# Interleaving two tensors: from two load buffers and two output buffers to three regions woven in place

## The chip, the core and the metric

The kernel runs on one core of one Trainium2 chip. The metric is device time in microseconds (us) for one execution of the program, lower is better.

Five engines work beside each other on a core. Here VectorE (DVE in the profile) copies; SyncE (SP) and ScalarE (ACT) issue transfers, each on a queue of its own; 16 DMA engines move the data between the chip's memory (HBM) and SBUF, the on-chip memory with 128 partitions. PSUM is a second, smaller on-chip memory. The engines are held in order by semaphores: an instruction waits until a counter has reached a value, and a transfer that has landed adds 16.

## What is computed

```python
# x, y: (32, 256, 1024) float32
result = np.zeros((32, 256, 2048), dtype=np.float32)
result[..., 0::2] = x
result[..., 1::2] = y
```

Nothing is calculated. Each output row takes its even places from x and its odd places from y. Both inputs hold 33.55 MB, the output 67.11 MB, so 134.22 MB have to cross between HBM and SBUF.

## The kernel before

x, y and the output are seen as flat lists of numbers. They are cut into n = 8 tiles. A tile of x is 128 partitions by W = 8192 numbers, a row of 32 KiB in each partition (4 MiB together); a tile of y is the same, and a tile of the output is 128 by 16384 numbers. Because interleaving keeps the order of the flat lists, tile k of the output needs tile k of x and of y alone, and partition p needs nothing of other partitions.

Six buffers of 32 KiB a partition fill 192 KiB: `xt[0]` and `xt[1]` for x, `yt[0]` and `yt[1]` for y (tile k uses number k % 2), and `ot[0]` and `ot[1]` for the output. An output buffer holds half of an output tile: `ot[0]` always the first half (h = 0), `ot[1]` the second (h = 1).

Three lists of instructions run beside each other:

- **SP issues the loads** (lines 42 to 53). Tile 0 of x comes in two halves (lines 42 and 43), so that copying can begin earlier. Then, for each k, x into `xt[k % 2]` (line 50) and y into `yt[k % 2]` (line 53). From k = 2 on, each waits until VectorE has made its last copy out of that buffer for tile k - 2 (the semaphore `woven`, lines 48 and 52).
- **VectorE weaves** (lines 55 to 70). For each half of a tile there are two copies of 4096 numbers a partition: x into the even places of `ot[h]` (line 67), y into the odd places (line 70). The first copy waits for the load of x and for the store of the same half of the tile before, since that store still reads `ot[h]` (line 64); the second copy of half 0 waits for the load of y.
- **ACT issues the stores** (lines 72 to 83), one of 4 MiB for each half, with rows of 32 KiB, after the two copies of that half. The first store of all is cut into a piece of 1 MiB with rows of 8 KiB (line 77) and one of 3 MiB with rows of 24 KiB (line 81).

At the end ACT waits for the last store of half 0 and clears the semaphores with one instruction over their range (line 90), and SP waits for the last store of half 1 and takes its count back (line 91).

The wrapper `tile_interleave_kernel` moves the first two loads on SP ahead of a drain in the opening block, so that they start early. It is the same in both kernels.

Of the kernel before, what the change touches and what calls it, by code (L numbers as in the profile page):

```python
# [3 lines left out]


def _interleave(nc, x, y, out):
    P = 128
    W = 8192
    H = W // 2  # L10

    total = 1
    for s in x.shape:
        total *= s
    n = total // (P * W)
    assert n * P * W == total

    def rows(ap, names, k):
        flat = ap.rearrange("b s d -> (b s d)")
        return flat[k * names : (k + 1) * names].rearrange("(p w) -> p w", p=P)  # L20

    fp32 = mybir.dt.float32
    xt = [nc.alloc_sbuf_tensor(f"xt{b}", [P, W], fp32).ap() for b in (0, 1)]
    yt = [nc.alloc_sbuf_tensor(f"yt{b}", [P, W], fp32).ap() for b in (0, 1)]
    ot = [nc.alloc_sbuf_tensor(f"ot{b}", [P, W], fp32).ap() for b in (0, 1)]

    xsem = [nc.alloc_semaphore(f"xsem{b}") for b in (0, 1)]
    hsem = nc.alloc_semaphore("hsem")
    qsem = nc.alloc_semaphore("qsem")
    ysem = [nc.alloc_semaphore(f"ysem{b}") for b in (0, 1)]  # L30
    woven = nc.alloc_semaphore("woven")
    osem = [nc.alloc_semaphore(f"osem{b}") for b in (0, 1)]


    cuts = [0, W // 4, W]
    parts = [slice(a, b) for a, b in zip(cuts, cuts[1:])]

    xs = [rows(x, P * W, k) for k in range(n)]
    ys = [rows(y, P * W, k) for k in range(n)]
    os_ = [rows(out, 2 * P * W, k) for k in range(n)]  # L40

    nc.sync.dma_start(out=xt[0][:, :H], in_=xs[0][:, :H]).then_inc(xsem[0], 16)
    nc.sync.dma_start(out=xt[0][:, H:], in_=xs[0][:, H:]).then_inc(hsem, 16)

    for k in range(n):
        b = k % 2
        if k >= 2:
            nc.sync.wait_ge(woven, 4 * (k - 2) + 3)
        if k:
            nc.sync.dma_start(out=xt[b], in_=xs[k]).then_inc(xsem[b], 16)  # L50
        if k >= 2:
            nc.sync.wait_ge(woven, 4 * (k - 2) + 4)
        nc.sync.dma_start(out=yt[b], in_=ys[k]).then_inc(ysem[b], 16)

    for k in range(n):
        b = k % 2
        for h in (0, 1):
            c = slice(h * H, (h + 1) * H)
            if h == 0:
                nc.vector.wait_ge(xsem[b], 16 * (k // 2 + 1))  # L60
            elif k == 0:
                nc.vector.wait_ge(hsem, 16)
            if k:
                nc.vector.wait_ge(osem[h], 16 * k)
            if (k, h) == (1, 0):
                nc.vector.wait_ge(qsem, 16)
            nc.vector.tensor_copy(out=ot[h][:, 0::2], in_=xt[b][:, c]).then_inc(woven, 1)  # L67
            if h == 0:
                nc.vector.wait_ge(ysem[b], 16 * (k // 2 + 1))
            nc.vector.tensor_copy(out=ot[h][:, 1::2], in_=yt[b][:, c]).then_inc(woven, 1)  # L70

    for k in range(n):
        for h in (0, 1):
            nc.scalar.wait_ge(woven, 4 * k + 2 * h + 2)
            if (k, h) == (0, 0):
                for c in parts[:-1]:
                    nc.scalar.dma_start(
                        out=os_[k][:, c], in_=ot[h][:, c]
                    ).then_inc(qsem, 16)
                c = parts[-1]  # L80
                nc.scalar.dma_start(out=os_[k][:, c], in_=ot[h][:, c]).then_inc(osem[h], 16)
                continue
            nc.scalar.dma_start(
                out=os_[k][:, h * W : (h + 1) * W], in_=ot[h]
            ).then_inc(osem[h], 16)

    nc.scalar.wait_ge(osem[0], 16 * n)
    used = sorted(s.num for s in [*xsem, hsem, qsem, *ysem, woven, osem[0]])
    assert used == list(range(used[0], used[-1] + 1)), used
    nc.scalar.sem_clear(range(used[0], used[-1] + 1))  # L90
    nc.sync.nop(nofuse=True).wait_op(osem[1], 16 * n, "sem-ge").then_inc(
        osem[1], -16 * n
    )


def kernel(tc, x, y, out):
    nc = tc.nc
    tc.close()
    tc.compile()

    _interleave(nc, x, y, out)

    blocks = nc.main_func.blocks
    for engine in (mybir.EngineType.SP, mybir.EngineType.SP):
        opening = blocks[0].instructions
        at, moved = next(
            (b, i)
            for b in blocks[1:]
            for i in b.instructions
            if i.engine == engine and i.opcode == "DMACopy"  # L110
        )
        assert not (moved.sync_info and moved.sync_info.on_wait)
        body = at.instructions
        body.remove(moved)
        gate = next(
            n
            for n, i in enumerate(opening)
            if i.engine == engine and i.opcode == "Drain"
        )
        opening.insert(gate, moved)  # L120
        at.instructions = body
        blocks[0].instructions = opening


# [1 line left out]
_INS = ['x', 'y']  # L126
_OUTS = [((32, 256, 2048), 'float32')]


# [23 lines left out]
```

## Time and profile before

| | |
|---|---|
| time, median of 3 runs | 314.25 us (314.22 to 314.38) |
| span of the profiled execution, first to last instruction | 312.9 us |
| what the median has over this span | 1.35 us |
| VectorE busy | 72.0 us (23% of the span) in 32 copies |
| DMA | 134.22 MB, 429 GB/s over the span |
| VectorE waited for stores | 206.5 us in 14 waits |
| VectorE waited for the first loads | x 7.3 us, y 12.3 us |

The profiled execution is a separate one, taken with the hardware profiler. Its durations are set against its own span of 312.9 us; the third row says what lies around it in an unprofiled run.

How to read the profile. An engine is busy while an instruction of its own works; instructions that only wait, branch or issue a transfer don't count. The page cuts the span into 40 equal slices of 7.8 us, and a digit gives the busy share in tenths (9 is 90% or more); the DMA row is the mean over the 16 DMA engines. The chain of work that ended last is followed backwards from the last instruction: at each step to what it had waited for. A DMA in that chain stands from its issue to its landing, so it may include time in which it stood in the queue behind others. A line of the timeline reads: start, duration, engine, line of the kernel, operation, target and source, and in brackets how long the engine was idle before and what ended that. A line of the DMA issues reads: target and source, issuing queue, number of issues, KB each, and the median time from issue to landing. Beside these views the trace keeps a record of every single DMA packet, with its start, duration and bytes; a packet here is one row of one partition.

### The profile page before, as it was taken

The page shows a single profiled execution, that of the slowest core. Times are in us where ns is not written, and L with a number is a line of the kernel's source. Part 1 is how long each engine was busy: PE and PEld are TensorE (multiplying, and loading weights), DVE is VectorE, ACT ScalarE, POOL GpSimd, SP SyncE. Part 2 cuts the span into 40 slices and gives each one's busy share as a digit, 9 for nine tenths or more (in the row PEclk, how much of TensorE's full clock was granted, in tenths as well). Part 3 has the DMA queues.
Part 4 walks back from the last instruction along what each step waited for, and adds up shares of the span by engine and source line. Part 5 has one row for each costly group of instructions (what it writes and reads, how often), then busy time and mean ns, then how long its engine had stood idle before and what let it go on. Part 6 is the DMA issues. An engine that isn't in the chain of part 4 may idle for free.

```text
span 312.9 us, 114 instructions
## 1 busy us (share of the span) xinstructions
DVE 72.0 (23%) x32; POOL 0.2 (0%) x4
## 2 busy tenths in 40 slices
DVE  0216000501305023050220503205032050415410
POOL 0000000000000000000000000000000000000000
DMA  8999999999999999999999999999999999999998
GB/s 337 467 402 436 436 402 419 452 457 415 427 444 411 461 402 469 402 469 402 469 402 465 406 440 432 423 448 402 469 402 469 402 469 402 469 402 448 423 423 381
DMA packets 4896, 134.22 MB, mean 429 GB/s; under 512 B 544, under 2 KB 544, under 8 KB 544
## 3 DMA queue, kind: packets, MB, share of 16 engines
q1 hardware_dynamic: 2448, 67.11, 50.1%
q10 hardware_dynamic: 2448, 67.11, 49.7%
HBM read 67.11 MB, written 67.11 MB: 429 GB/s over the span
## 4 chain that ended last, share of the span: by engine, by line
DMA 82%; DVE 12%; issue 0%
DMA out_dram<-ot 76%; DMA yt<-in_y_dram 6%; DVE ot L70 6%; DVE ot L67 6%
## 5 line engine op out<-in xcount | busy, mean ns | idle before, releaser
L67 DVE COPY ot<-xt 128x4096 f32<-128x4096 f32 x16 | 36.7, 2295 | 213.8 <-DMA out_dram<-ot 206.5
L70 DVE COPY ot<-yt 128x4096 f32<-128x4096 f32 x16 | 36.6, 2288 | 12.3 <-DMA yt<-in_y_dram 12.3
L137 POOL MEMSET const-bfloat16-1.0<- 128x1 bf16 x1 | 0.1, 103 | 0.0
L137 POOL MEMSET const-uint8-127<- 128x1 uint8 x1 | 0.1, 102 | 0.0
L137 POOL MEMSET const-float32-0.0<- 128x1 f32 x1 | 0.1, 100 | 0.2 <-issue 0.2
L137 POOL MEMSET const-float32-1.0<- 128x1 f32 x1 | 0.1, 99 | 0.0
## 6 DMA issues: line engine op xcount, KB each, us to landing
out_dram<-ot ACTq DMA_DIRECT2D x15, 4096.0 KB, 34.1
yt<-in_y_dram SPq DMA_DIRECT2D x8, 4096.0 KB, 41.5
xt<-in_x_dram SPq DMA_DIRECT2D x7, 4096.0 KB, 24.3
xt<-in_x_dram SPq DMA_DIRECT2D x2, 2048.0 KB, 9.5
out_dram<-ot ACTq DMA_DIRECT2D x1, 3072.0 KB, 32.8
out_dram<-ot ACTq DMA_DIRECT2D x1, 1024.0 KB, 16.3
```

Source lines behind the costliest of these rows:

```text
L67: nc.vector.tensor_copy(out=ot[h][:, 0::2], in_=xt[b][:, c]).then_inc(woven, 1)
L70: nc.vector.tensor_copy(out=ot[h][:, 1::2], in_=yt[b][:, c]).then_inc(woven, 1)
L137: nc = _bacc.Bacc("TRN2", target_bir_lowering=False, num_devices=1)
```

## The change

The six buffers become three regions `R[0]` to `R[2]` of 64 KiB a partition, 192 KiB together; tile k uses region k % 3. x of a tile is loaded into the first half of its region, y into the second half, and the output tile is woven in the same 64 KiB. So that nothing is overwritten before it is read, the second half of x (4096 numbers a partition) is first parked in PSUM. The rest of the weaving is a chain of copies, each of which waits for the one before (the semaphore `step`):

1. the second half of x to PSUM (`park`);
2. the first half of x spread over the even places of the first half of the region, in pieces from the top: 2048, 1024, 512, 256, 128 and 64 numbers, and then the last 64 by way of a small buffer `last`, 8 copies;
3. the first half of y into the odd places of the first half of the region: one copy. The first half of the output tile is now done;
4. the second half of y spread over the odd places of the second half, in such pieces from the bottom, 8 copies;
5. the parked half of x from PSUM into the even places of the second half.

That is 19 copies a tile, where there were 4. Loads of a region wait until all of the stores of the tile that had it have landed. Stores have rows of 64 KiB for tiles 1 to 4 (one transfer of 8 MiB, after all 19 copies). Tiles 5, 6 and 7 are stored in two halves with rows of 32 KiB, the first one after step 3. Tile 0 is stored in three parts, with rows of 8, 24 and 32 KiB. Both halves of tile 0 of x have to be in before the first copy. The semaphores are cleared one at a time.

The core of the diff (the names of buffers and semaphores at the head are left out):

```diff
+    def copy(to, of):
+        nonlocal count
+        if count:
+            nc.vector.wait_ge(step, count)
+        nc.vector.tensor_copy(out=to, in_=of).then_inc(step, 1)
+        count += 1
+    def halvings(m):
+        while m > 64:
+            assert m % 2 == 0
+            yield m // 2, m
+            m //= 2
+        yield 0, m
...
     for k in range(n):
-        b = k % 2
-        if k >= 2:
-            nc.sync.wait_ge(woven, 4 * (k - 2) + 3)
+        b = k % REGIONS
+        X = low = R[b][:, :N]
+        Y = high = R[b][:, N:]
+        if k == 0:
+            nc.vector.wait_ge(fsem, 16)
+        nc.vector.wait_ge(xsem[b], 16 * (k // REGIONS + 1))
+        copy(park, X[:, H:])
+        for i, j in halvings(H):
+            if i:
+                copy(low[:, 2 * i : 2 * j : 2], X[:, i:j])
+            else:
+                copy(last[:, :j], X[:, :j])
+                copy(low[:, 0 : 2 * j : 2], last[:, :j])
+        nc.vector.wait_ge(ysem[b], 16 * (k // REGIONS + 1))
+        copy(low[:, 1::2], Y[:, :H])
+        halves = [count]
+        for i, j in halvings(H):
+            i, j = H - j, H - i
+            if j < H:
+                copy(high[:, 2 * i + 1 : 2 * j : 2], Y[:, H + i : H + j])
+            else:
+                copy(last[:, : j - i], Y[:, H + i : H + j])
+                copy(high[:, 2 * i + 1 : 2 * j : 2], last[:, : j - i])
+        copy(high[:, 0::2], park)
+        done.append(halves + [count])
...
+        cuts = [0, 2 * N]
+        if k == 0:
+            cuts = [0, N // 4, N, 2 * N]
+        elif k >= n - 3:
+            cuts = [0, N, 2 * N]
+        for c, d in zip(cuts, cuts[1:]):
+            stores.append((k, slice(c, d), done[k][d > N]))
+            stored[b] += 16
...
+    for k in range(n):
+        b = k % REGIONS
+        if free[k]:
+            nc.sync.wait_ge(ssem[b], free[k])
         if k:
-            nc.sync.dma_start(out=xt[b], in_=xs[k]).then_inc(xsem[b], 16)
-        if k >= 2:
-            nc.sync.wait_ge(woven, 4 * (k - 2) + 4)
-        nc.sync.dma_start(out=yt[b], in_=ys[k]).then_inc(ysem[b], 16)
+            nc.sync.dma_start(out=R[b][:, :N], in_=xs[k]).then_inc(xsem[b], 16)
+        nc.sync.dma_start(out=R[b][:, N:], in_=ys[k]).then_inc(ysem[b], 16)
...
+    for k, c, ready in stores:
+        b = k % REGIONS
+        nc.scalar.wait_ge(step, ready)
+        nc.scalar.dma_start(out=os_[k][:, c], in_=R[b][:, c]).then_inc(ssem[b], 16)
...
+    for s in [*xsem, fsem, *ysem, step, *clear]:
+        nc.scalar.sem_clear(range(s.num, s.num + 1))
```

More of the change, by code (lines that the diff above doesn't have):

```diff
@@ L14, in _interleave @@
         total *= s
-    n = total // (P * W)
-    assert n * P * W == total
+    n = total // (P * N)
+    assert n * P * N == total
     def rows(ap, names, k):
         flat = ap.rearrange("b s d -> (b s d)")
-        return flat[k * names : (k + 1) * names].rearrange("(p w) -> p w", p=P)
+        size = names * P * N
+        return flat[k * size : (k + 1) * size].rearrange("(p w) -> p w", p=P)
     fp32 = mybir.dt.float32
-    xt = [nc.alloc_sbuf_tensor(f"xt{b}", [P, W], fp32).ap() for b in (0, 1)]
@@ L24, in _interleave @@
[L24 to L43, printed above, removed]
-    for k in range(n):
-        b = k % 2
-        if k >= 2:
-            nc.sync.wait_ge(woven, 4 * (k - 2) + 3)
-        if k:
-            nc.sync.dma_start(out=xt[b], in_=xs[k]).then_inc(xsem[b], 16)
-        if k >= 2:
-            nc.sync.wait_ge(woven, 4 * (k - 2) + 4)
-        nc.sync.dma_start(out=yt[b], in_=ys[k]).then_inc(ysem[b], 16)
@@ L55, in _interleave @@
[L55 to L92, printed above, removed]
+    R = [nc.alloc_sbuf_tensor(f"R{b}", [P, 2 * N], fp32).ap() for b in range(REGIONS)]
+    last = nc.alloc_sbuf_tensor("last", [P, 64], fp32).ap()
+    park = nc.alloc_psum_tensor("park", [P, H], fp32).ap()
@@ new lines, in _interleave @@
+    xsem = [nc.alloc_semaphore(f"xsem{b}") for b in range(REGIONS)]
+    fsem = nc.alloc_semaphore("fsem")
+    ysem = [nc.alloc_semaphore(f"ysem{b}") for b in range(REGIONS)]
+    step = nc.alloc_semaphore("step")
+    ssem = [nc.alloc_semaphore(f"ssem{b}") for b in range(REGIONS)]
+    xs = [rows(x, 1, k) for k in range(n)]
+    ys = [rows(y, 1, k) for k in range(n)]
+    os_ = [rows(out, 2, k) for k in range(n)]
+    count = 0
+    def copy(to, of):
[4 more added lines that the diff above has]
+        count += 1
@@ new lines, in _interleave @@
+    stores = []
+    stored = [0] * REGIONS
+    free = []
+    for k in range(n):
+        b = k % REGIONS
+        free.append(stored[b])
+        cuts = [0, 2 * N]
[6 more added lines that the diff above has]
+            stored[b] += 16
+    nc.sync.dma_start(out=R[0][:, :FIRST], in_=xs[0][:, :FIRST]).then_inc(fsem, 16)
@@ new lines, in _interleave @@
+    nc.sync.dma_start(out=R[0][:, FIRST:N], in_=xs[0][:, FIRST:]).then_inc(xsem[0], 16)
+    for k in range(n):
+        b = k % REGIONS
+        if free[k]:
+            nc.sync.wait_ge(ssem[b], free[k])
+        if k:
+            nc.sync.dma_start(out=R[b][:, :N], in_=xs[k]).then_inc(xsem[b], 16)
+        nc.sync.dma_start(out=R[b][:, N:], in_=ys[k]).then_inc(ysem[b], 16)
+    for k, c, ready in stores:
+        b = k % REGIONS
+        nc.scalar.wait_ge(step, ready)
+        nc.scalar.dma_start(out=os_[k][:, c], in_=R[b][:, c]).then_inc(ssem[b], 16)
@@ L93, in _interleave @@
+    final = (n - 1) % REGIONS
+    clear = [s for b, s in enumerate(ssem) if b != final]
+    for b in range(REGIONS):
+        if b != final:
+            nc.scalar.wait_ge(ssem[b], stored[b])
+    for s in [*xsem, fsem, *ysem, step, *clear]:
+        nc.scalar.sem_clear(range(s.num, s.num + 1))
+    nc.sync.nop(nofuse=True).wait_op(ssem[final], stored[final], "sem-ge").then_inc(
+        ssem[final], -stored[final]
     )
```

7 lines of the change are left out of this document (5 added, 2 removed).

## The prediction

> **What bounds the kernel now.** I read the page's DMA rows first, then the chain of work that ended last, then the DMA issues, then the timeline.
>
> ```profile
> span 312.9 us, 114 instructions
> ...
> DVE 72.0 (23%) x32; POOL 0.2 (0%) x4
> ...
> DMA  8999999999999999999999999999999999999998
> ...
> DMA packets 4896, 134.22 MB, mean 429 GB/s; under 512 B 544, under 2 KB 544, under 8 KB 544
> ...
> q1 hardware_dynamic: 2448, 67.11, 50.1%
> q10 hardware_dynamic: 2448, 67.11, 49.7%
> ...
> DMA 82%; DVE 12%; issue 0%
> ```
>
> The reader should see that the 16 DMA engines are busy in every slice but the first and the last, half of it for loads (q1) and half for stores (q10). The chain also gives 12% to VectorE (DVE), but that does not mean 12% could be won: while those copies run, the DMA row does not fall. The timeline shows what a turn of the loop takes:
>
> ```profile
> 76.83 2.29 DVE L67 COPY ot<-xt 128x4096 f32<-128x4096 f32 x1 [14.76 <-DMA out_dram<-ot]
> ...
> 115.55 2.29 DVE L67 COPY ot<-xt 128x4096 f32<-128x4096 f32 x1 [14.75 <-DMA out_dram<-ot]
> ...
> 283.90 2.30 DVE L67 COPY ot<-xt 128x4096 f32<-128x4096 f32 x1 [8.95 <-DMA out_dram<-ot]
> ...
> 293.53 2.29 DVE L67 COPY ot<-xt 128x4096 f32<-128x4096 f32 x1 [5.14 <-DMA out_dram<-ot]
> ```
>
> One tile takes 115.55 - 76.83 = 38.72 us and moves four transfers of 4.19 MB: **T = 9.68 us** for each. Near the end, with loads over, a store lands 293.53 - 283.90 = 9.63 us after the one before. So loads beside stores and stores alone move at the same rate. All 134.22 MB are 32 such units, 32 x 9.68 = 309.8 us, and the span is 3.1 us more: the start and the landing of the end. The bound is bytes, and no stage has a hole. The bytes stay the same, so the change can win only the per-row and per-transfer cost, and can lose only where it leaves both queues empty.
>
> **How the two queues share.** The order of landings decides whether a hole opens, so I need the rule of sharing.
>
> ```profile
> out_dram<-ot ACTq DMA_DIRECT2D x1, 3072.0 KB, 32.8
> out_dram<-ot ACTq DMA_DIRECT2D x1, 1024.0 KB, 16.3
> ```
>
> The 1 MiB piece of the first store has rows of 8 KiB, and runs beside loads with rows of 32 KiB. Shared by bytes it would take twice its own 2.42 us, 4.8 us. Row for row, five times its bytes move, 12.1 us. The packet records of the trace have its first row moving at 28.64, 4.40 us after its issue at 24.24; 12.1 + 4.4 = 16.5 against 16.3 shown. The 3 MiB piece (24 KiB rows, 7.26 us alone) gets 24 parts of 56: 16.9 us; it was issued at 24.64 and, behind the first, has 16.3 us up to 57.4. So the queues alternate **by row, not by bytes**.
>
> **The parts.**
>
> 1. Rows of 64 KiB (tiles 1 to 4). No packet of the trace is that long. The packet records give 309 ns for 8 KiB, 611 for 16, 912 for 24, 1213 for 32: 301 to 302 ns for each 8 KiB plus 7 to 8 ns a row. The near price is 1213 + 4 x 301 = 2417 ns, 9 ns under two rows of 32 KiB. The far ends are no loss or gain (2426), and the dearest rate per byte that is shown, 8 x 309 = 2472, 46 ns over. An engine has 8 such rows in each of 4 tiles: 32 x 9 = **-0.3 us**, ends -0.3 and +1.5. I take the near price, since four rows lie on that line. The four transfers fewer (34 become 30) save 16 packets of a few bytes each; by the 9 ns that the records have for one, under 0.1 us in all.
>
> 2. VectorE. Four copies of 2.29 us per tile become 19 in a chain, each with a wait on the one before. L67 and L70 start 2.21 us apart when not held, 0.54 ns an element. The halvings of one half are 8 copies with 4160 elements in all: 2.25 us, plus a fixed cost each. The trace has one size of VectorE copy, so that fixed cost lies between nothing and the whole 2.29. I take 0.2: the nearest small operations are the four 0.10 us memsets of the page, to which I add 0.08 (2.29 - 2.21) and the 0.02 that the chain shows between a landing and a copy. That is 3.85 us for each half. The two parking copies go through PSUM, which this trace doesn't show: 2.29 by the nearest row, 9.2 if four times as slow; I take 4.6, on the dear side. A tile is then 4.6 + 3.85 + 2.3 + 3.85 + 4.6 = 19.2 us, eight tiles 154 us, half of the span. What hides it is DMA work of 38.72 us a tile. After y has landed, the low half is ready 2.3 us later, the high half 8.45 after that.
> The Trainium skill, "VectorE: DVE Perf Modes", section "Why PSUM operands drop a tier", says that a copy with an operand in PSUM and fp32 data loses the two-port mode, so goes one element a cycle. No run here shows it; with that page's cycle table the estimate is (120 + 4096)/0.96 = 4.39 us a parking copy, and the tile would be 18.8 us.
>
> 3. Waits. On SP the loads of tile k+3 wait for all of store k; only later loads queue behind. On ACT each store waits for a count of copies; later stores queue behind, which go out in that order anyway. SP issues seven loads at the start (five before); nothing waits behind them. ACT clears its semaphores one by one, in the last tile's store (19.4 us). I cost these at nothing; the landing times below are what covers them.
>
> **Walk through the landings.** Time and work keep step at T a unit from 3.1 us, as long as one queue has rows. The first store starts at 24.24 now: y's landing at 21.9 plus one low copy. In the new kernel x of tile 0 is folded by about 21 (x in at 12.2 by the trace's landings, then 8.45 us), so the low copy comes at the same time, and until 57.6 the same transfers lie in the same two queues.
> - 57.6: (57.6 - 3.1)/9.68 = 5.63 units, one of them a store; 1.37 of the six first loads are left. The other half of store 0, row for row: 2 T, to 76.9; 0.37 loads left.
> - Store 1, 64 KiB rows beside 32 KiB rows: 2 units of its own and 1 of loads, 29.0 us, to 105.9; store 2 likewise to 135.0. Tile 2 was in at 87.6 and woven by 99. Of tile 3's loads 0.63 and then 1.63 are done.
> - **The store queue runs dry**: tile 3 is in at 138.6, and its store can move 12.2 us later (landing 0.4, the copies 10.75, about 1.0 from issue to first row, as for the first load), at 150.8. The loads fill this: the regions of tiles 1 and 2 are free. Store 3 ends at about 180, store 4 at about 214, with a second dry stretch of 5 us under loads.
> - Store 5 goes out in halves: y in at 216.0, low half moving 3.7 us later (0.4 + 2.3 + 1.0), with 0.38 of tile 6 loaded meanwhile. Then four store transfers stand against 3.62 loads, row for row: the last y lands at 219.7 + 3.62 x 19.36 = 289.8, and 0.38 of store 6, 3.7 us, is left, just what tile 7's low half needs. Store 7 moves from 293.5, two units: **312.9**. The high half is woven 8.45 us after the low one, plus 1.0 to its first row: inside the 9.68 us that the low store takes.
>
> The balance at the end is no accident: the stretch that the store queue is dry before store 5 is the same chain (landing, one copy, issue) that must be covered before store 7. In the middle it is longer, since a new store's first row stood 4.4 us behind loads (28.64 - 24.24), and at the end there are none to stand behind. That puts about 3.4 us into the cover.
>
> **Sum.** Span 312.9 - 0.3 (rows) - 0.0 (waits) = 312.6; the median of the runs, 314.25, lies 1.35 us over the span of the profiled execution, so **314.0 us**, no measurable change. A difference under 0.2% (0.63 us) can't be told from none.
>
> **Rivals.**
> - *The last weave lies bare* (slower): store 6 is done before y of tile 7 lands, or the high half comes after the low store. It decides when the cover is under 3.7 us for the low half, or the high half's 8.45 + 1.0 goes over 9.68: a fixed cost of 0.23 instead of 0.2 us in each of 8 copies would do that if the low store started without delay. Price: from nothing to the whole 3.7, so up to 317.7. For it: the walk has the low half's cover at exactly its need. Against: the 3.4 us above. 0.12.
> - *64 KiB rows cost more* (slower): at the 8 KiB rate, 314.25 + 1.5 = 315.8. Against: the straight line of four sizes. 0.06.
> - *VectorE becomes the bound* (slower): with 2.29 us for each of 19 copies, 43.5 us a tile is over 38.72, and 8 x 43.5 = 348 us and more. Nothing in the trace excludes it but the 0.10 us of small memsets, on another engine. 0.02.
> - *A cost per transfer that the change saves* (faster). If transfers paid a gap of their own, four fewer would show; stores landing 9.63 us apart, under the 9.68 of a unit in the mix, leave no gap to save. What is left is the lost time outside the 32 units, 3.1 us; a third of it gone would give 313.2. 0.08. The Trainium skill, "DMA: Bandwidth & Descriptors", section "Anatomy of one DMA", fits 2.0 us a transfer plus bytes at 436 GB/s, 11.6 us for 4.19 MB; by that four fewer are worth 8 us, 306.2. The 9.63 us contradict it for transfers that stand in a queue.
> - *The change doesn't do what it says*: rows of 64 KiB are cut to 32 KiB on the way. Then sharing is equal, store and load in step, the cover at the end longer: 314.25. It is inside the forecast.
>
> **How the numbers follow.** Forecast 0.72, between 313.6 and 314.9. Faster 0.08, slower 0.20 (0.12 + 0.06 + 0.02). The range goes from 313.3 (a little into the faster case) to 316.5 (dear rows, and the bare weave up to two thirds of its price); the rest, under 2 in 10, lies out.
>
> **What would show it.** Right: 9 in every slice of the DMA row but the ends; single packets of 64 KiB near 2417 ns; stores 1 to 4 about 29 us beside loads, with idle waits of ACT between tiles 2 and 5; the last two stores 9.7 us apart. Wrong: a DMA slice under 9 between the first and last, above all near 290; a VectorE copy of 64 elements far over 0.2 us; a span longer than 313.5 with no hole, which would mean dearer rows.

## The result and the profile after

The changed kernel takes **323.73 us** (median of 4 runs, 322.85 to 324.59) against 314.24 us before: 1.0301 times the time, 95% interval 1.028 to 1.0322. It was forecast at 314.0 us, no change. It also scatters: the four runs of the kernel before lie within 0.3 us, those of the changed one within 1.8. The views below are of the execution of 322.85 us, the fastest of the four. Medians here are over all runs and ratios over the means of the fast ones; only e5, below, has a run that counts as slow, of 330.47 us.

The page of the kernel after, in the lines that answer to those of before:

```profile
span 321.5 us, 249 instructions
...
DVE 144.6 (45%) x152; POOL 0.2 (0%) x4
...
DMA  8999999999999999999999899999999999997897
...
DMA packets 4321, 134.23 MB, mean 417 GB/s; under 512 B 480, under 2 KB 480, under 8 KB 480
...
q14 instruction: 1, 0.01, 0.0%
```

Two things are new in these rows. The DMA engines are not full in slice 23 (177 us) and in slices 37 and 38 (289 to 305 us), and the last slice is a little emptier than before. And there is a third queue with a single packet: 8 KiB of instructions, fetched in the run at 80.0 us by the packet records.

The table of stages, of the kernel before and then of the one after (stretch, its length, busy VectorE and GpSimd with the number of instructions, granted clock, mean busy share of the DMA engines, GB/s):

```profile
77.40:135.50 58.10, 13.39 (x7) 0.00 (x0) 1.00 1.00 433
135.50:154.90 19.40, 4.65 (x3) 0.00 (x0) 1.00 1.00 432
154.90:193.60 38.70, 8.97 (x5) 0.00 (x0) 1.00 1.00 434
193.60:232.30 38.70, 8.96 (x5) 0.00 (x0) 1.00 1.00 434
232.30:290.40 58.10, 17.42 (x8) 0.00 (x0) 1.00 1.00 433
290.40:300.10 9.70, 4.50 (x2) 0.00 (x0) 1.00 1.00 432
```

```profile
77.40:135.50 58.10, 18.08 (x19) 0.00 (x0) 1.00 1.00 433
135.50:154.90 19.40, 12.41 (x11) 0.00 (x0) 1.00 1.01 434
154.90:193.60 38.70, 15.85 (x19) 0.00 (x0) 1.00 1.00 422
193.60:232.30 38.70, 16.16 (x19) 0.00 (x0) 1.00 0.99 397
232.30:290.40 58.10, 27.89 (x29) 0.00 (x0) 1.00 1.01 434
290.40:300.10 9.70, 2.84 (x2) 0.00 (x0) 1.00 0.63 270
```

Up to 155 us the rate is that of before, although tiles 1 and 2 go out in 64 KiB rows. From 155 to 232 us the engines are busy all the time, but move 422 and then 397 GB/s: their packets take longer than before. From 290 to 300 us over a third of the engine time is empty. The two terms can be summed from the packet records: for every packet, its duration less the ordinary one of its size (2418 ns for 64 KiB, 1213 for 32 KiB, and so on), divided by 16 engines; and the time that the engines stand empty after 285 us.

```
us per engine          slow rows   empty after 285 us   last row ends
before                    1.18            0.06              312.48
after                     5.33            4.36              321.01
difference                4.15            4.30                8.53
```

The two terms, 8.45 us, account for the 8.53 us by which the last row of this execution ends later. Where they come from shows in the landings. A transfer is counted in 16 steps, one from each engine. This is the time of the last of them and how long before it the first one came, by the landing records of the trace:

```
landing of       y2     store 1  store 2  x4      y4      y5      y7      store 6 (2nd half)
last, us         88.6   108.1    138.4    151.8   174.1   223.7   297.2   302.1
first earlier by  1.2     2.6      3.9     3.9    14.1    11.3    16.5      8.1
```

Before, no landing spreads over more than 0.5 us. Here one single engine falls back after 80 us, the other 15 stay within 0.4 us until 152; at y4 that one is 14.1 us late, and the others have split up too, into six and nine that land 2.2 us apart. At the end the engines that are ahead have moved all that there is by 294 us and stand empty, while those behind still bring the last y. The timeline shows what that holds up:

```profile
297.23 5.58 DVE L47 COPY R<-R 128x4096 f32<-128x4096 f32 x7 [11.23 <-DMA R<-in_y_dram]
299.55 8.54 ACTq L115 DMA_DIRECT2D out_dram<-R  x2
```

VectorE waited for y of tile 7 until 297.2, and the last tile's first half was issued at 299.6.

The packet records don't name the engine. But a row begins within a few ns of the end of another, so the rows can be joined into 16 chains, one for each engine. In them the fetch begins at 79.97 us, as one engine's row ends; that engine's next row begins when the fetch ends, and takes 1744 ns in place of 1213. Together it is 0.31 + 0.53 = 0.84 us behind the other 15.

### The profile page after: what moved, and what is told of

The parts are those of the page before. It is cut to its first block, busy times and chain, and to the rows that moved or that the text cites. A ratio compares the mean times of both kernels' runs of the same rounds, so it can differ in the third digit from the quotient of the medians.

```text
span 321.5 us, 249 instructions
## 1 busy us (share of the span) xinstructions
DVE 144.6 (45%) x152; POOL 0.2 (0%) x4
## 4 chain that ended last, share of the span: by engine, by line
DMA 33%; DVE 32%; another core or an unknown queue 29%; issue 1%; DVEq 0%
DVE R L47 24%; DMA out_dram<-R 14%; DMA R<-in_x_dram 13%; DVE park L47 7%; DMA R<-in_y_dram 6%; DVE last L47 1%; DVEq L46 0%
## 5 line engine op out<-in xcount | busy, mean ns | idle before, releaser
L47 DVE COPY R<-R 128x2048 f32<-128x2048 f32 (+6 forms) x104 | 67.5, 649 | 88.7 <-DMA R<-in_y_dram 85.4
L47 DVE COPY park<-R 128x4096 f32<-128x4096 f32 x8 | 35.4, 4428 | 73.1 <-DMA R<-in_x_dram 73.0
L47 DVE COPY R<-park 128x4096 f32<-128x4096 f32 x8 | 35.4, 4425 | 0.3
L47 DVE COPY R<-last 128x64 f32<-128x64 f32 x16 | 3.2, 197 | 0.5
L47 DVE COPY last<-R 128x64 f32<-128x64 f32 x16 | 3.1, 195 | 0.6
```

What stands on the lines that cost most here:

```text
L47: nc.vector.tensor_copy(out=to, in_=of).then_inc(step, 1)
```

## The experiments

Theories that the expectations speak of. A: the instruction fetch sets one engine back, and the alternation of 64 KiB with 32 KiB rows multiplies its lag. B: 64 KiB rows lose time by themselves. C: the chain of copies and the wait for whole stores lose it. D: rows are slower where some engines load while others store. E: every return of the store queue from a dry stretch (a time in which it has no row to move) throws engines out of step. F: that takes rows of two lengths.

**e1: the changed kernel with 32 KiB rows.** The stores of tiles 1 to 4 go out in two transfers each, both still after all 19 copies.

```diff
+        elif k:
+            cuts = [0, N, 2 * N]
         for c, d in zip(cuts, cuts[1:]):
-            stores.append((k, slice(c, d), done[k][d > N]))
+            whole = 0 < k < n - 3
+            stores.append((k, slice(c, d), done[k][whole or d > N]))
```

> The changed kernel with stores of tiles 1 to 4 in two transfers of 32 KiB rows, both still after all 19 copies; the 152 copies, the waits and the fetch of instructions stay. Theory A (one DMA engine is held up by an instruction fetch near 80 us, and alternation of 64 KiB with 32 KiB rows multiplies its lag): the lag stays at about one row (1 to 4 us between the first and the last engine of a landing) and is not multiplied, 314 to 316 us. Theory B (64 KiB rows beside 32 KiB rows lose time by themselves, the fetch is a bystander): 314.0 to 314.6 us. Theory C (the loss is in the long chain of VectorE copies and the wait of loads for whole stores): 322 to 324 us, as with the change.

Measured: 315.23 us, 1.0031 (1.0019 to 1.0043). The fetch is there, at 79 us; one engine falls back by 1.1 us, and by the end 1.9, no more. Slow rows cost 0.1 us after 77 us. So C falls, and nearly all of the loss needs the long rows. (With long rows a tile is also stored in one transfer of 8 MiB in place of two of 4; the two were not told apart.)

**e2: fewer copies.** The spreading ends at 1024 numbers in place of 64.

```diff
-    last = nc.alloc_sbuf_tensor("last", [P, 64], fp32).ap()
+    last = nc.alloc_sbuf_tensor("last", [P, 1024], fp32).ap()
...
-        while m > 64:
+        while m > 1024:
```

> The changed kernel with the spreading ended at 1024 numbers in place of 64 (a small buffer of 4 KiB a partition): 11 copies a tile, 88 in all in place of 152, rows of 64 KiB and all waits kept. Theory A: with the shorter program no instruction fetch falls into the run, all 16 engines land within 0.5 us of each other to the end, 314.0 to 315 us. Theory B: the fetch does not matter, 321 to 325 us. Theory C: the chain after y is 1.5 us shorter in each half, at most 12 us of copies less in the run but the same waits: 320 to 323 us.

Measured: 320.76 us, 1.0195 (1.0158 to 1.0232). The fetch is still there, but at 155 us. Until 148 us all landings lie within 0.4 us, so the 64 KiB rows of tiles 1 and 2 cost nothing at all; then engines fall apart, 2.5 us at 171, 8.4 at 253. Between theories A and B: less loss, not none. The time lies in the range of C, which e1 had excluded.

**e3: the kernel before with a long list of copies.** 17 copies of one number a partition behind each tile's four.

```diff
+        for _ in range(17):
+            nc.vector.wait_ge(padsem, pads)
+            nc.vector.tensor_copy(
+                out=pad[:, pads : pads + 1], in_=pad[:, pads - 1 : pads]
+            ).then_inc(padsem, 1)
+            pads += 1
```

> The kernel before with 136 VectorE copies of one number a partition added, 17 behind each tile's four copies, so that its program is as long as the changed one's. Theory A: the instruction fetch is there and holds one engine up by a row, but stores and loads alternate in rows of one length and the store queue is never dry, so the lag is not multiplied: 314.2 to 315.8 us. The rival that a fetch in the run costs by itself, whatever the rows: 318 us or more. Theory B and C: 314.2 us.

Measured: 315.42 us, 1.0037 (1.0022 to 1.0051). The fetch comes at 101 us; from there one engine lands 1.0 us behind the first, 1.2 at the end. By the chains of rows it is the engine that moved the fetch: its next row takes 1746 ns in place of 1213. So a fetch by itself costs about 1 us: what one engine is behind is added to the last landing.

**e4: e2 and one row more.** One extra load of 8 KiB, on one partition and so on one engine, ahead of tile 3.

```diff
+        if k == REGIONS:
+            nc.sync.dma_start(out=spare, in_=xs[0][0:1, :2048]).then_inc(pokesem, 16)
```

> The kernel with 88 copies and rows of 64 KiB, and one extra load of a single row of 8 KiB on SP ahead of the load of tile 3 (issued near 77 us), which one DMA engine has to move: a stand-in for the instruction fetch. Theory A: one engine falls behind, its lag is multiplied, 318 to 325 us. Theory B: same as without that load, 321 to 325 us with or without. If 88 copies alone give about 314 us and this one does too, the lag of one engine isn't the cause.

Measured: 325.15 us, 1.035 (1.0325 to 1.0374). One row, 0.3 us of one engine's time, costs 4.4 us more than e2: landings spread over 7.5 us by 124 us, and 24.7 us by 281.

**e5 and e6: the fetch moved forward.** To e2, 48 small copies are added ahead of the first tile; e6 has the extra row of e4 too.

```diff
+    for i in range(PADS):
+        nc.vector.wait_ge(padsem, i + 1)
+        nc.vector.tensor_copy(out=pad[:, i + 1 : i + 2], in_=pad[:, i : i + 1]).then_inc(
+            padsem, 1
+        )
```

> The kernel with 88 copies and rows of 64 KiB, with 48 copies of one number a partition added ahead of the first tile, while VectorE would wait for x anyway: the same instruction fetch is expected, but before 25 us, when loads run alone. Theory A (the fetch sets one engine back while both queues alternate, and 64 KiB rows beside dry stretches multiply that lag): landings stay within 0.6 us of each other, 313.9 to 314.8 us. Theory B (64 KiB rows lose time by themselves): 318 to 322 us, as with 88 copies alone. Theory A with a fetch that hurts at any time: 318 to 325 us.

> The same with the early fetch, and one extra load of a single 8 KiB row on SP ahead of the load of tile 3, near 77 us. Theory A: this one row alone, with no fetch later, brings the loss back: 318 to 325 us, with one engine's landings late by 5 us and more. Theory B or a fetch that does something other than take an engine's turn: the same time as the kernel with the early fetch alone, within 0.7 us.

Measured: 328.66 us, 1.0416 (1.035 to 1.0482), and 328.71 us, 1.0456 (1.044 to 1.0472). The fetch came at 24.9 us. That it would be harmless there was wrong: the engine stayed 0.9 us behind, 1.5 at 89 us, 5.5 at 140. That e6 equals e5 doesn't clear the extra row; the engines are out of step in both, and in both the spread reaches 24 us and more.

**e7 and e8: small rows in the kernel before.** Six extra loads of 8 KiB rows, on eight engines or on all 16.

```diff
+            if k > 2:
+                nc.sync.wait_ge(pokesem, 16 * (k - 2))
+            nc.sync.dma_start(out=spare, in_=xs[0][0:8, :2048]).then_inc(pokesem, 16)
```

> The kernel before (all rows 32 KiB) with six extra loads of 8 rows of 8 KiB, one ahead of each of the loads of tiles 2 to 7, so that eight of the 16 engines are set back a little more with each tile and the rows of loads and stores no longer change over at the same time on all engines. The extra bytes cost 6 x 0.3 = 1.8 us on those eight engines. Theory D (packets are slower when some engines read HBM while others write): packets over 1.3 us show up and the time goes over 317 us. The rival (mixed phases cost nothing with 32 KiB rows; slow packets need 64 KiB rows): 315.5 to 316.5 us.

> The control: the kernel before with six extra loads of 16 rows of 8 KiB, one row on each of the 16 engines, so that all are set back alike. Both theories: 6 x 0.3 = 1.8 us more than before and no slow packets, 315.8 to 316.4 us. If the one with eight engines is over this by 1 us or more, mixed phases cost time; if it is equal, they don't.

Measured: 323.05 us, 1.0277 (1.026 to 1.0294), and 321.88 us, 1.0255 (1.0187 to 1.0322). The control failed: with the same extra row on all 16 engines they did not stay together either. The spread of e8's landings grew as the small rows came, 0.8 us at 50 us, 1.3 at 91, 2.0 at 170, 3.2 at 189, 5.5 at 228 and 11.5 at 281, with 1.6 us of slow rows after 77 us and 7.1 us empty at the end. The chains show how it begins: at 47.6 us the 24 KiB row that follows the small one takes 912 ns on one engine and up to 1360 on others. So the pair doesn't decide on D. But it shows a loss of that size without 64 KiB rows, where rows of another length are put between.

**e9 and e12: fewer copies still.** The spreading ends at 2048 numbers, 72 copies in all; in e12 the copy of y into the first half is not held by the one before.

```diff
-        while m > 64:
+        while m > 2048:
...
-        copy(low[:, 1::2], Y[:, :H])
+        copy(low[:, 1::2], Y[:, :H], held=False)
```

> The changed kernel with the spreading ended at 2048 numbers: 9 copies a tile, 72 in all. The fetch came at about the 57th instruction of VectorE's list in the four kernels so far that have it, which is here at the start of tile 5, near 197 us. Theory A (the fetch sets one engine back, and only then do 64 KiB rows lose time): no slow rows and landings within 0.6 us up to 190 us, and less loss than with the fetch at 155 us: 315 to 318.5 us. Theory B (64 KiB rows lose time by themselves): slow rows from 77 or 150 us on, 319 to 325 us.

> As with 72 copies, but the copy of y into the first half waits for the landing of y alone and not for the copy before it, which saves one waiting instruction a tile: by the same count the fetch moves to about 217 us, behind the last transfer with rows of 64 KiB. Theory A: all four 64 KiB stores run without a slow row, and the fetch meets rows of 32 KiB only: 314.2 to 316 us. Theory B: 319 to 325 us.

Measured: 319.67 us, 1.0178 (1.0155 to 1.0201), and 319.97 us, 1.0169 (1.011 to 1.0228). In both the fetch came at 188 us (217 was expected of e12), and both lose step before it. In e12 x of tile 4 lands within 0.3 us at 148.3, and y of tile 4, the first load beside the store that comes back from the dry stretch, spreads over 3.1 us at 170.5: 12 engines early, four late. In the stages of e12:

```profile
154.90:193.60 38.70, 12.91 (x8) 0.00 (x0) 1.00 0.99 419
193.60:232.30 38.70, 18.52 (x9) 0.00 (x0) 1.00 1.00 423
...
290.40:300.10 9.70, 5.54 (x4) 0.00 (x0) 1.00 0.73 314
```

So theory A fell as the only cause. Both times lie in the range given for B, but the rows of tiles 1 and 2 cost nothing in e12 (2418 ns each, all 256), so long rows alone are not it either. The fetch isn't needed: the return of the store queue at 152.6 us does it as well. By the chains of rows, the first store row is ready while the engines change from one load row to the next: four engines begin it at 152.55 to 152.72 us, the other 12 have just begun one more load and follow at 153.73 to 153.85. At y of tile 4 those four are one 64 KiB row behind.

**e10: the fetch before all stores.** As e5, with 64 small copies in front in place of 48.

> The kernel with 88 copies and 64 small copies in front in place of 48, so that the fetch comes near 10 us, long before the first store. If an engine that is set back while loads run alone keeps its lag (theory A, at any time): 320 to 331 us, as with the fetch at 25 us. If the lag is taken up before the stores begin: landings within 0.6 us and 314 to 315.5 us.

Measured: 323.28 us, 1.0286 (1.0242 to 1.033). The fetch came at 13.9 us; by 59 us two engines were apart from the rest, 2.2 us, and the spread went to 18.4 us.

**e11: 32 KiB rows and 72 copies**, each half stored as soon as it is woven.

> Three regions woven in place with 32 KiB rows in all stores of tiles 1 to 7, the first half of each stored as soon as it is woven, and 9 copies a tile. With rows of one length a lag of one engine isn't multiplied: 314.2 to 315.5 us, the lag after the fetch 1 to 2 us. Theory C (regions, waits and the long chain cost time by themselves): 318 us or more.

Measured: 314.88 us, 1.002 (1.001 to 1.0029), with 0.05 us of slow rows after 77 us. The fetch at 178 us leaves one engine 1.1 us behind until the end.

**e13, e14, e15: which of the two, dry stretch or long rows?** All have e11's copies. e13 has 32 KiB rows and a forced dry stretch; e14 has 64 KiB rows for tile 1 alone (`elif k > 1`), which leaves no dry stretch; e15 for tiles 1 and 2 (`elif k > 2`), and the store comes back from its dry stretch with 32 KiB rows.

```diff
         nc.scalar.wait_ge(step, ready)
+        if k == 3 and c.start == 0:
+            nc.scalar.wait_ge(xsem[2], 32)
```

> The kernel with 32 KiB rows and 72 copies (314.88 us), but the store of tile 3 waits until x of tile 5 has landed, so that the store queue is dry from about 154 to 168 us while loads run alone, with rows of one length before and after. Theory E (any return of the store queue from a dry stretch puts engines a row apart, and rows are then slow): landings spread by 1.2 us and more from 168 us on, slow rows, 316 to 320 us. Theory F (it takes rows of two lengths at the return): landings within 0.6 us until the fetch and 1.2 us after it, 314.6 to 315.6 us.

> The same kernel without the forced wait, with rows of 64 KiB in the store of tile 1 alone. Loads then fall back by one transfer, less than the lead they have, so the store queue never runs dry. Theory E and theory F: no step is lost, 314.5 to 315.4 us. Theory B (64 KiB rows lose time by themselves, dry or not): slow rows from 77 us on, 315.8 us or more.

> Rows of 64 KiB in the stores of tiles 1 and 2, then 32 KiB. The store queue runs dry once, near 135 us, and comes back with rows of 32 KiB, in halves. Theory E: engines fall apart at that return, near 142 us, spread 1.2 us and more, 316 to 319 us. Theory F: the return is with rows of one length, so landings stay within 0.6 us until the fetch, 314.6 to 315.6 us.

Measured: 315.03 us, 1.0026 (1.0015 to 1.0037); 314.84 us, 1.0018 (1.0009 to 1.0028); 314.93 us, 1.0024 (1.0014 to 1.0033). In e15 no store row moved from 133 to 145 us, and the landings behind that lie within 0.3 us until the fetch at 188. In e13 the spread is 0.2 us at 167.6, the last landing before the store queue returns at 171.8. The fetch follows at 173.1, so the two can't be told apart there; the spread is 1.0 us then, and later up to 2.2, where 1.2 was expected, and still the time is within 0.8 us of before. So B and E fall as stated: neither the long rows nor the dry stretch costs anything alone. F fits all three times: it takes an engine out of step **while** long rows stand beside short ones.

One limit of this the chains show. Neither return put engines out of step by itself: in e15 all 16 begin the first store row within 0.25 us (145.10 to 145.35), in e13 none takes one more load first. In e12 four and 12 parted there, and in the changed kernel nine and six (155.97 to 156.24 and 157.14 to 157.42 us). Whether a return parts them seems to hang on the moment at which it falls, which no run sets on purpose. That a lag doesn't grow with rows of one length rests on the lag from the fetch, in e1, e3 and e11.

The landing spread (the widest in each stretch) beside the two terms, by the trace. Each line is one execution, and those of e2 (318.61 us), e4 (326.30) and e12 (321.27) lie 1.2 to 2.2 us from their medians:

```
                  fetch   spread, us, at landings of         slow rows    empty after
                  at us   77-149   149-200   200-303 us     after 77 us   285 us
before              -       0.3      0.2       0.3             0.00          0.1
e11 rows 32 KiB    178      0.3      1.1       1.1             0.05          0.7
e14 one long       188      0.3      1.0       1.0             0.05          0.7
e15 two long       188      0.3      1.1       1.1             0.05          0.9
e13 dry, 32 KiB    173      0.3      1.0       2.2             0.20          0.6
e12 four long      188      0.3      9.1      12.1             3.09          4.1
e2  four long      155      0.3      7.0       8.4             1.21          3.4
after               80      3.9     14.1      16.7             4.25          4.4
e4  extra row      160      7.5     17.7      24.7             2.02         10.3
e5  early fetch     25      5.5     18.3      24.0             8.65          5.3
```

## Why the prediction was wrong, point by point

- **What bounds the kernel: right.** Bytes through 16 DMA engines. No time was won there: the best of the three-region kernels (e14, 314.84) is 0.6 us slower than before.
- **Sharing by row: right.** The first engine to finish store 1 does so at 105.5 us, store 2 at 134.5, y of tile 3 at 138.1, against 105.9, 135.0 and 138.6 in the walk.
- **The price of a 64 KiB row: right for an engine in step**, 2418 ns against 2417. Of the 256 such rows from 150 to 232 us the mean is 2556 ns, the slowest 4034, over the far end of the range (2472). That end was taken from the rows of the kernel before, where the engines are in step.
- **VectorE: right.** The groups of the page after:

```profile
L47 DVE COPY R<-park 128x4096 f32<-128x4096 f32 x8 | 35.4, 4425 | 0.3
L47 DVE COPY R<-last 128x64 f32<-128x64 f32 x16 | 3.2, 197 | 0.5
L47 DVE COPY last<-R 128x64 f32<-128x64 f32 x16 | 3.1, 195 | 0.6
```

 A small copy is busy for 0.20 us, and the eight copies of a half took 3.75 us in the last tile (3.85 was taken); a parking copy takes 4.43 (4.6). In all 144.6 us busy against 154. The Trainium skill, "VectorE: DVE Perf Modes", section "Why PSUM operands drop a tier", had given an estimate of 4.39 us, which the row bears out within 1%.
- **The step that failed: "Time and work keep step at T a unit from 3.1 us, as long as one queue has rows".** The walk took 16 engines for one. By the chains of rows each engine takes turns between its own two queues, and a landing is the landing of the slowest: 14.1 us after the first at y of tile 4, 16.5 at y of tile 7. Two things put an engine out of step, and neither was in the walk: the fetch of instructions that a list of 152 copies brings into the run (0.84 us on one engine), for which the prediction had no term; and the return of the store queue from the dry stretch, which the walk counted as harmless.
- **Why a lag is multiplied**: at 152 us the late engine is 3.9 us behind, 3.2 rows of 1.21 us, all of them loads. When the store comes back, each of these rows waits for a 64 KiB row, 1.21 + 2.42 = 3.63 us a turn. The chains show it: the late engine's loads begin at 159.16, 162.78, 166.40 and 170.10 us with a 64 KiB row between each two, while nine others begin their last row of y at 158.4 to 158.7. As a sum, 3.2 x 3.63 = 11.7, and one such row more is 14.1, the spread at y of tile 4. The Trainium skill, "DMA: Bandwidth & Descriptors", section "Why a DMA increments its semaphore by 16 and not by 1", says that the engines finish independently and that only the full count tells that all has landed; the landing records agree, with 14.1 us between the first and the last of the 16 steps.
- **The balance at the end.** It was argued that the cover of the last weave equals its need. By the first engine, y of tile 7 lands at 280.7 us, by the last at 297.2 (289.8 in the walk), and the engines ahead run empty from 294. So the rival "the last weave lies bare" did happen, 4.3 us against its price of 3.7 at most; but the point from which it decides was not a cost of the copies. It was the spread of the engines.
- **The rival "64 KiB rows cost more"** was priced at 1.5 us; slow rows took 4.15. But the length alone isn't it: after 77 us the 64 KiB rows lost 2.35 us and the 32 KiB rows 1.90, single ones up to 2.8 us long. Why a row is slow when engines are out of step is **open**. In e12, for instance, all 256 rows of tiles 1 and 2, in step, have 2418 ns, and rows of 3.8 us stand in the record at 170 us, the first stage out of step. The experiment meant to tell whether loads beside stores do it (e7 against e8) had a control that fell out of step itself. So about half of the loss, the empty engines at the end, is traced to its cause, and the other half only to the state in which it arises.
- **The other rivals** did not happen. VectorE was busy for 45% of the span, and 512 rows of 64 KiB moved whole. Fewer transfers gained nothing: e11 with 34 of them took 314.88 us, e14 with 33 314.84, e15 with 32 314.93. The fit of 2.0 us a transfer that the prediction quotes from the Trainium skill, "DMA: Bandwidth & Descriptors", section "Anatomy of one DMA", is headed there as that of transfers issued by GpSimd; here SP and ACT issue them.

## What to carry to other kernels

When the DMA engines are the bound, treat them as 16 machines that can fall out of step. One length of row in both queues kept the spread to 1 to 2.2 us in each kernel tried without small rows put between. Long rows beside short ones cost nothing while the engines were in step (e14, e15), and let a small lag grow to a spread of 8 to 27 us where they were not. Before trusting a walk through two queues, read the first and the last step of each landing, not only the last. And a longer list of instructions is itself DMA traffic on one engine.

## What the runs showed of the hardware

- One packet of 8 KiB of instructions, 309 ns on one engine, costs the kernel before 1.2 us (e3, 315.42 against 314.26), as the engine that moved it lands 1.0 to 1.2 us behind to the end. More than the fetch itself is the row behind it, 1746 ns in place of 1213. It appeared once in each kernel whose VectorE list had 72 copies or more, when 44 to 63 of them had started, and in none with 32. That it is VectorE's is concluded from its moving with that list. The Trainium skill, "Runtime: NRT & Kernel Launch", section "Instruction fetch mechanics", calls the cost of passing from one fetched block of instructions to the next mostly hidden. For VectorE the trace of e2 agrees: its copies run on across the fetch at 155.0 us, one starting 0.04 us after the other's end. For the kernel bound by DMA it isn't hidden, by the 1.2 us of e3.
- Engines out of step are not always slow: the changed kernel moves 434 GB/s from 232 to 290 us, in rows of 32 KiB and with a spread of 16 us. In e12 the same stage lost 1.3 us to slow rows.
